# Up stages of two feed-forwards with the activations stationary and 512 weight columns moving

## Chip, cores and metric

One core of one Trainium2 chip. The metric is the device time of one execution in microseconds; the medians below are over runs of the same program.

## What is computed

One encoder layer on 256 tokens of width 2048 in float32: a SwiGLU feed-forward, token mixing by two kinds of attention heads, a second feed-forward. Each part has a normed and modulated input (adaLN) and a gated residual. The change touches the two feed-forwards:

```python
def swiglu(x, w_gate, w_up, w_down):
    return (jax.nn.silu(x @ w_gate) * (x @ w_up)) @ w_down

mod = jax.nn.silu(c) @ w_ada[l] + b_ada[l]
f = swiglu(modulate(rms_norm(h, g_ffn1[l]), sh1, sc1), w1_gate[l], w1_up[l], w1_down[l])
h = h + 0.5 * gt1[:, None, :] * f
```

D_FF is 5632; `w_gate` and `w_up` are 2048 x 5632, `w_down` 5632 x 2048, `w_ada` 2048 x 18432. 501 MB are read from HBM, all weights once.

## The kernel before

**Numbers.** A float32 matrix product is made of three fp32r products. Each operand is split in a high half (a cast to fp32r) and a low half (the rest). `mm3` (L212) issues high x high, high x low and low x high into the same PSUM bank; `mm2` (L217) does the same in two matmuls, the first of 512 columns that hold the high and the low half of the moving operand, the second of 256.

**The weight stream.** `Flow` (L50) streams all weights of the layer in the order of their use, in chunks of 128 x 1024 floats (512 KB): `fetch` issues the DMA on SP's queue (4 buffers), `to_hi` casts on ACT (L84, tile `hiw`, 4 buffers), `to_lo` subtracts on DVE (L91, tile `low`, 3 buffers). `step` (L114) is one chunk: high half of chunk u+3, low half of chunk u+2, then the events registered for this chunk (phase 0), then adaLN jobs, then the events of phase 1. What `step` returns is chunk u, on which PE works next. `fl.at(d, fn)` registers work for the d-th step from the coming one. So the order on each engine is written out by hand.

**adaLN jobs.** The 9 x 2048 values of `mod` are dot products on DVE (L186, 1024 columns of `w_ada` in each). They run beside the other work: at each step the credit grows by the rate of the stage (`RATE_A` to `RATE_H`), and for each whole credit one job runs, if its load has been issued (3 buffers). `pace` sets the rate and puts the credit to zero.

**Feed-forward.** The 16 k tiles of the input (`nh[k]`, `nl[k]`, 128 x 256: high and low half of the activations, channels on partitions) become ready one after another, so the sum over k is split in passes (SPLIT1 = 3, 8, 16; SPLIT2 = 4, 10, 16). `up_start` (L355) does the first k tiles for 8 f tiles, with all eight PSUM banks. `up_pass` (L370) runs over the f tiles (128 of D_FF each, FT = 44): per f one PSUM bank `pu` with gate in columns 0 to 255 and up in 256 to 511, per k one `mm3` for each. The stationary operand is the 128 x 128 block of weights, the moving one are the 256 tokens, and the result has D_FF on partitions. The first pass copies it to `part` (`keep`, ACT), the later ones add it there (DVE, L381). After the last pass `silu_soon` (L337) makes tanh (ACT), two products (DVE, L343 and L344), the high half (ACT) and the low half (DVE) of the hidden activations `hd`, one step after another. `ffn_down` (L388) takes them as the moving operand: per output tile 44 blocks, `mm2` each.

**Where the other form stands already.** `qkv_unit` (L556) has the activations stationary (128 tokens of `nh[k]`) and 512 columns of weights moving, with `mm3`; tokens are then on partitions.

```python
for t in range(2):
    ts_ = slice(t * P, (t + 1) * P)
    mm3(ps[t], nh[k][:, ts_], nl[k][:, ts_], whi[:, sl], wlo[:, sl],
        k == 0, k == KT - 1)
```

Transposes on PE stand in the attention heads (L646 and L688): a block of 128 x 128 float32 against `ident`.

Of the kernel before, what the change touches and what calls it, by code (L numbers as in the profile page):

```python
# [9 lines left out]
F32 = mybir.dt.float32  # L10
# [18 lines left out]
NF0 = 8  # L29
# [3 lines left out]
RATE_B = 0.66  # L33
RATE_C = 0.28
RATE_D = 0.97
# [14 lines left out]
class Flow:  # L50
# [63 lines left out]
    def step(self):  # L114
        u = self.u
        self.to_hi(u + LOOK + 1)
        self.to_lo(u + LOOK)
        self.run(0)
        self.credit += self.rate
        while self.credit >= 1.0 and self.fetched:  # L120
            self.credit -= 1.0
            self.job()
        self.run(1)
        self.u += 1
        return self.hi.pop(u), self.lo.pop(u)

    def next(self):
        if self.blk == 8:
            self.w = self.step()
            self.blk = 0  # L130
        sl = slice(self.blk * P, (self.blk + 1) * P)
        self.blk += 1
        return self.w[0][:, sl], self.w[1][:, sl]
# [7 lines left out]
def build(tc, a):  # L141
    nc = tc.nc
    with ExitStack() as ctx:
# [77 lines left out]
        def split_hi(src, hi):  # L221
            nc.scalar.copy(hi, src)
# [7 lines left out]
        def rstd_tiles(w, tag):  # L230
            return [sp.tile([P, w], F32, tag=f"{tag}{i}", bufs=(2 if i == 2 else 1), name=f"{tag}{i}") for i in range(3)]
# [18 lines left out]
        class Stat:  # L250
# [7 lines left out]
            def square(self, t, on_dve=False):  # L258
                sq = sp.tile([P, S], F32, tag="sq", bufs=3, name="sq")
                if on_dve:  # L260
                    nc.vector.tensor_tensor(sq, t, t, ALU.mult)
                else:
                    nc.scalar.activation(sq, t, AF.Square)
                return sq
# [60 lines left out]
        part, hid, pairs = {}, {}, {}  # L325

        def pair_tile(hp, kind, f, dt):
            key = kind, f // 2
            if key not in pairs:
                pairs[key] = hp.tile([P, 2, 2, S], dt, tag="hid", name=f"{kind}{f // 2}")  # L330
            return pairs[key][:, f % 2]

        def keep(hp, f, ps):
            part[f] = pair_tile(hp, "pt", f, F32)
            nc.scalar.copy(part[f], ps)  # L335

        def silu_soon(hp, f, d):  # L337

            g_, u_ = part[f][:, 0, :], part[f][:, 1, :]
            th = sp.tile([P, S], F32, tag="nt", bufs=4, name="th")  # L340

            def e1():
                nc.vector.scalar_tensor_tensor(th, th, 1.0, g_, ALU.add, ALU.mult)  # L343
                nc.vector.scalar_tensor_tensor(th, th, 0.5, u_, ALU.mult, ALU.mult)  # L344

            def e2():
                hid[f] = pair_tile(hp, "hd", f, F32R)
                split_hi(th, hid[f][:, 0, :])

            fl.at(d, lambda: nc.scalar.activation(th, g_, AF.Tanh, scale=0.5))  # L350
            fl.at(d + 1, e1)
            fl.at(d + 2, e2)
            fl.at(d + 3, lambda: split_lo(th, hid[f][:, 0, :], hid[f][:, 1, :]))

        def up_start(hp, K, before):  # L355
            pa = [bank(f"pa{f}").rearrange("p (j s) -> p j s", j=2) for f in range(NF0)]
            for k in range(K):
                for j in range(2):
                    whi, wlo = before(k, j)
                    assert k in normed  # L360
                    for b in range(8):
                        f, q = 4 * j + b // 2, b % 2
                        sl = slice(b * P, (b + 1) * P)
                        mm3(pa[f][:, q, :], whi[:, sl], wlo[:, sl], nh[k], nl[k],
                            k == 0 and q == 0, k == K - 1 and q == 1, skip_group_check=True)
                    if k == K - 1:
                        for f in range(4 * j, 4 * j + 4):
                            fl.at(0, lambda f=f: keep(hp, f, pa[f]))

        def up_pass(hp, f0, k0, k1, kind):  # L370
            for f in range(f0, FT):
                ps = bank("pu").rearrange("p (j s) -> p j s", j=2)
                for j in range(2):
                    for k in range(k0, k1):
                        w = fl.next()
                        assert k in normed, (f, k)
                        mm3(ps[:, j, :], *w, nh[k], nl[k], k == k0, k == k1 - 1)
                if kind == "first":
                    fl.at(0, lambda f=f, ps=ps: keep(hp, f, ps))
                else:  # L380
                    fl.at(0, lambda f=f, ps=ps: nc.vector.tensor_tensor(part[f], part[f], ps, ALU.add))  # L381
                    if kind == "last":
                        silu_soon(hp, f, 1)
# [32 lines left out]
        hp = hps.enter_context(tc.tile_pool(name="hid1", bufs=FT // 2 + 1))  # L416
        K1 = SPLIT1[0]

        def big(nm):
            return hp.tile([P, 4, S], F32, tag="hid", name=nm)  # L420
# [6 lines left out]
        def early_load(k):  # L427
            for j in (1, 0):
                for b in range(2):
                    early[k, j, b] = big("ra").rearrange("p a s -> p (a s)")  # L430
                    nc.sync.dma_start(early[k, j, b], a["w_ada"][j * KT + k, b])
# [5 lines left out]
        for k in range(1, K1):  # L437
            early_load(k)
            fl.fetch(min(2 * k + 1, RAWW - 1))
        for b in range(2):  # L440
            th = big("thc").rearrange("p a s -> p (a s)")
            cs = slice(b * CW, (b + 1) * CW)
            nc.scalar.activation(th, cb[:, cs], AF.Tanh, scale=0.5)
            nc.vector.scalar_tensor_tensor(cb[:, cs], th, 1.0, cb[:, cs], ALU.add, ALU.mult)
# [8 lines left out]
        for q in range(4):  # L453
            sq = big("sq1")
            nc.scalar.activation(sq, h4[q], AF.Square)
            for i in range(4):
                nc.tensor.matmul(ps1, ones, sq[:, i, :], start=q + i == 0, stop=q + i == 6)
# [29 lines left out]
        up_pass(hp, NF0, 0, K1, "first")  # L487
# [11 lines left out]
        pairs.clear()  # L499
# [268 lines left out]
        hp2 = ctx.enter_context(tc.tile_pool(name="hid2", bufs=FT // 2 + 1))  # L768
# [12 lines left out]
        up_pass(hp2, NF0, 0, K2, "first")  # L781
# [11 lines left out]
def _consts():  # L793
# [25 lines left out]
    "w1_s": (SPLIT1[0] * 2, P, CW), "w1_a": ((FT - NF0) * 2 * SPLIT1[0] // 8, P, CW),  # L819
    "w1_b": (FT * 2 * (SPLIT1[1] - SPLIT1[0]) // 8, P, CW),  # L820
    "w1_c": (FT * 2 * (SPLIT1[2] - SPLIT1[1]) // 8, P, CW), "w1_d": (KT * FT // 8, P, CW),
    "w2_s": (SPLIT2[0] * 2, P, CW), "w2_a": ((FT - NF0) * 2 * SPLIT2[0] // 8, P, CW),
# [7 lines left out]
def _arrays(inputs):  # L830
# [23 lines left out]

    arr["c"] = c(g["c"].reshape(2, CW))
    for l, cuts in ((1, SPLIT1), (2, SPLIT2)):
        gu = np.stack([g[f"w{l}_gate"][0], g[f"w{l}_up"][0]]).reshape(2, KT, P, FT, P)
        gu = gu.transpose(3, 0, 1, 2, 4)
        arr[f"w{l}_s"] = stream(gu[:NF0, :, : cuts[0]].transpose(2, 0, 1, 3, 4))
        arr[f"w{l}_a"] = stream(gu[NF0:, :, : cuts[0]])  # L860
        arr[f"w{l}_b"] = stream(gu[:, :, cuts[0] : cuts[1]])
        arr[f"w{l}_c"] = stream(gu[:, :, cuts[1] :])
# [24 lines left out]
```

## Time and profile before

| | |
|---|---|
| median of 3 runs | 1968.88 us (1966.86 to 1969.74) |
| profiled execution | 1968.11 us |
| its span, first to last instruction | 1966.3 us |
| PE busy | 1925.8 us, 98% |
| DVE busy | 1557.6 us, 79% |
| ACT busy | 900.2 us, 46% |
| HBM read | 501.14 MB, 256 GB/s over the span |

The matmuls of PE overlap: the next begins before the last one has ended, and their ends are modelled. So the duration of one matmul is longer than its share of the time, and the share is read from start to start, or from the pieces of the chain of waits. The chain goes back from the last instruction to what released each, so it shows what sets the end. An arrow `<-` names the instruction that ended an idle time; "issue" means that the profile shows no wait.

### The profile page before, as it was taken

To read this page: it belongs to the slowest core of one execution; us is meant where nothing else is said; L and a number is where in the kernel's file an instruction comes from. 1 tells how busy PE (TensorE), PEld (TensorE's weight loads), DVE (VectorE), ACT (ScalarE), POOL (GpSimd) and SP (SyncE) were. 2 spreads that over 40 slices of the span, in tenths; PEclk is the share of its full clock that TensorE was granted. 3 is DMA by queue.
4 is the path that set the end of the run, shared out by engine and by line. 5 is a ranking of instruction groups with operands and counts; after the bars stand their busy time and mean duration, and the time that the engine had idled before them with its cause. 6 is when DMAs were issued, how large, how long until landed. Compare 5 with 4: busy or idle time off the path is not lost.

```text
span 1966.3 us, 34176 instructions
## 1 busy us (share of the span) xinstructions
PE 1925.8 (98%) x13552; PEld 1805.0 (92%) x13552; DVE 1557.6 (79%) x2238; ACT 900.2 (46%) x1299; POOL 0.7 (0%) x6
## 2 busy tenths in 40 slices
PE   5999999999999999999999999999999999999999
PEld 4999999999988888788888998999999999988887
DVE  5889987888899999778888988777777889876444
ACT  3653334444443334455555544554333555533332
POOL 0000000000000000000000000000000000000000
PEclk8999999999999999999999999999999999999999
DMA  8898886777799999676766646888777666786553
GB/s 310 310 337 305 309 299 233 236 240 237 229 327 373 365 370 361 206 237 215 250 204 205 209 166 224 293 290 265 257 254 260 216 220 218 223 281 235 195 192 127
DMA packets 141137, 505.48 MB, mean 257 GB/s; under 512 B 15664, under 2 KB 17968, under 8 KB 140976
## 3 DMA queue, kind: packets, MB, share of 16 engines
q1 hardware_dynamic: 140976, 503.30, 74.9%
q8 instruction: 106, 1.74, 0.3%
q14 instruction: 55, 0.45, 0.1%
HBM read 501.14 MB, written 2.10 MB: 256 GB/s over the span
## 4 chain that ended last, share of the span: by engine, by line
PE 95%; DVE 3%; DMA 2%; issue 0%; ACT 0%; SPq 0%; DVEq 0%; ACTq 0%
PE pd L218 17%; PE pu L213 17%; PE pu L215 17%; PE pu L214 17%; PE pd L219 9%; PE pqv L213 2%; PE pqv L214 2%; PE pqv L215 2%; PE pqk L213 2%; PE pqq L213 1%; PE pqk L215 1%; PE pqq L215 1%; PE pqk L214 1%; PE pqq L214 1%; PE pso L213 1%; PE pso L215 1%
## 5 line engine op out<-in xcount | busy, mean ns | idle before, releaser
L84 ACT CAST hiw<-rw 128x1024 fp32r<-128x1024 f32 x656 | 691.9, 1056 | 997.2 <-PE pu L214 359.8
L91 DVE TENSOR_TENSOR low<-rw,hiw 128x1024 fp32r<-128x1024 f32 x656 | 802.4, 1224 | 346.7 <-issue 128.8
L213 PE MATMUL pu<-nx,hiw 128*128 128x256 f32 x2704 | 765.3, 283 | 0.2 <-ACT pt L335 0.2
L215 PE MATMUL pu<-nx,low 128*128 128x256 f32 x2704 | 765.2, 283 | 0.0
L214 PE MATMUL pu<-nx,hiw 128*128 128x256 f32 x2704 | 765.2, 283 | 0.0
L213 PEld LDWEIGHTS pu<-nx,hiw 128*128 128x128 f32 x2704 | 519.2, 192 | 0.4 <-ACT pt L335 0.4
L215 PEld LDWEIGHTS pu<-nx,low 128*128 128x128 f32 x2704 | 519.2, 192 | 0.0
L214 PEld LDWEIGHTS pu<-nx,hiw 128*128 128x128 f32 x2704 | 519.2, 192 | 0.0
L218 PE MATMUL pd<-hd,hiw 128*128 128x512 f32 x1408 | 497.6, 399 | 0.0
L219 PE MATMUL pd<-hd,low 128*128 128x256 f32 x1408 | 395.5, 281 | 0.0
L218 PEld LDWEIGHTS pd<-hd,hiw 128*128 128x128 f32 x1408 | 264.6, 188 | 65.8
L219 PEld LDWEIGHTS pd<-hd,low 128*128 128x128 f32 x1408 | 266.0, 189 | 0.0
L186 DVE CUSTOM_DVE_ANT_0 ra<-ra,cb,acc 128x1024 f32<-128x1024 f32 x144 | 187.1, 1299 | 0.2
L381 DVE TENSOR_TENSOR pt<-pt,pu 128x512 f32<-128x512 f32 x176 | 119.8, 681 | 0.0
L186 DVE CUSTOM_DVE_ANT_0 ra<-ra,cb,vec 128x1024 f32<-128x1024 f32 x64 | 81.8, 1279 | 0.0
L213 PE MATMUL pso<-ox,hiw 128*128 128x256 f32 x256 | 72.3, 282 | 0.0
L215 PE MATMUL pso<-ox,low 128*128 128x256 f32 x256 | 71.4, 279 | 0.0
L214 PE MATMUL pso<-ox,hiw 128*128 128x256 f32 x256 | 71.4, 279 | 0.0
L186 DVE CUSTOM_DVE_ANT_0 ra<-ra,cb,gin 128x1024 f32<-128x1024 f32 x48 | 64.3, 1341 | 0.0
L213 PE MATMUL pqv<-hiw,nx 128*128 128x512 f32 x128 | 51.5, 402 | 3.5 <-ACT nx L297 3.5
L213 PE MATMUL pqk<-hiw,nx 128*128 128x512 f32 x128 | 51.4, 401 | 0.0
L213 PE MATMUL pqq<-hiw,nx 128*128 128x512 f32 x128 | 50.9, 397 | 0.0
(128 smaller groups left out, 1676.9 us busy)
## 6 DMA issues: line engine op xcount, KB each, us to landing
ra<-in_w_ada_dram SPq DMA_DIRECT2D x288, 512.0 KB, 5.0
rw<-in_w_d_dram SPq DMA_DIRECT2D x176, 512.0 KB, 4.8
rw<-in_w_c_dram SPq DMA_DIRECT2D x154, 512.0 KB, 4.2
rw<-in_w_b_dram SPq DMA_DIRECT2D x121, 512.0 KB, 4.6
rw<-in_w_qkv_dram SPq DMA_DIRECT2D x96, 512.0 KB, 4.2
rw<-in_w_a_dram SPq DMA_DIRECT2D x63, 512.0 KB, 4.7
rw<-in_w_o_dram SPq DMA_DIRECT2D x32, 512.0 KB, 3.6
rw<-in_w_s_dram SPq DMA_DIRECT2D x14, 512.0 KB, 3.8
```

What stands on the lines that cost most here:

```text
L84: self.nc.scalar.copy(t, self.raw[self.nhi])
L91: self.nc.vector.tensor_tensor(t, self.raw.pop(self.nlo), self.hi[self.nlo].bitcast(F32), ALU.subtract)
L186: nc.vector.tensor_tensor_reduce(out=raw, in0=raw, in1=cb[:, b * CW : (b + 1) * CW], scale=scale, scalar=init, op0=ALU.mult, op1=ALU.add, ...
L213: nc.tensor.matmul(out, lh, rh, start=first, stop=False, **kw)
L214: nc.tensor.matmul(out, lh, rl, start=False, stop=False, **kw)
L215: nc.tensor.matmul(out, ll, rh, start=False, stop=last, **kw)
L218: nc.tensor.matmul(ps, lh, r.rearrange("p t s -> p (t s)"), start=first, stop=False)
L219: nc.tensor.matmul(ps[:, :S], ll, r[:, 0, :], start=False, stop=last)
L381: fl.at(0, lambda f=f, ps=ps: nc.vector.tensor_tensor(part[f], part[f], ps, ALU.add))
```

## The change

Gate and up projections take the form that the q/k/v projection has. `wide3` multiplies 128 tokens (stationary) by 512 weight columns (moving), for both halves of the tokens; the four weight tiles of a group G share one such matmul, and gate and up (j = 0, 1) follow one another in two banks each. The weights are laid out for this on the host (`halves`). `part[G]` holds tokens on partitions: two halves of 512 columns, for gate and for up. `gate_soon` makes tanh and the first product as soon as gate is complete; `hid_soon` makes the second product (`e0`, DVE), turns it by eight transposes on PE into two banks `ph` (`e1`, in a new phase 3 of the step, just ahead of the chunk's matmuls), and splits it from there (`e2` on ACT, `e3` on DVE) into the same `hid[f]` as before, four f tiles in one tile. The down projection is as before. Tiles of the pool `hid` are twice as big and half as many; `sq` shares two buffers with tanh, and the tiles of `rstd_tiles` share `nt`. Three rates are changed.

```diff
-NF0 = 8
-RATE_B = 0.66
-RATE_C = 0.28
-RATE_D = 0.97
+RATE_B = 0.6
+RATE_C = 0.36
+RATE_D = 0.9
...
         self.run(1)
+        self.run(3)
         self.u += 1
...
+    def half(self):
+        w = self.blk
+        if w == 8:
+            self.w = self.step()
+            w = 0
+        self.blk = w + 4
+        sl = slice(w * P, (w + 4) * P)
         return self.w[0][:, sl], self.w[1][:, sl]
...
-            return [sp.tile([P, w], F32, tag=f"{tag}{i}", bufs=(2 if i == 2 else 1), name=f"{tag}{i}") for i in range(3)]
+            ts = [sp.tile([P, S], F32, tag="nt", bufs=4, name="rt")[:, :w] for i in range(2)]
+            return ts + [sp.tile([P, w], F32, tag=tag, bufs=2, name=tag)]
...
-                sq = sp.tile([P, S], F32, tag="sq", bufs=3, name="sq")
+                sq = sp.tile([P, 512], F32, tag="th", bufs=2, name="sq")[:, :S]
...
-        part, hid, pairs = {}, {}, {}
-
-        def pair_tile(hp, kind, f, dt):
-            key = kind, f // 2
-            if key not in pairs:
-                pairs[key] = hp.tile([P, 2, 2, S], dt, tag="hid", name=f"{kind}{f // 2}")
-            return pairs[key][:, f % 2]
-
-        def keep(hp, f, ps):
-            part[f] = pair_tile(hp, "pt", f, F32)
-            nc.scalar.copy(part[f], ps)
-
-        def silu_soon(hp, f, d):
-
-            g_, u_ = part[f][:, 0, :], part[f][:, 1, :]
-            th = sp.tile([P, S], F32, tag="nt", bufs=4, name="th")
+        part, hid = {}, {}
+
+        def wide3(ps, k, whi, wlo, first, last):
+            assert k in normed, k
+            for t in range(2):
+                ts_ = slice(t * P, (t + 1) * P)
+                mm3(ps[t], nh[k][:, ts_], nl[k][:, ts_], whi, wlo, first, last)
+
+        def keep(hp, G, j, ps):
+            if j == 0:
+                part[G] = hp.tile([P, 2, 2, 512], F32, tag="hid", name=f"pt{G}")
+            for t in range(2):
+                nc.scalar.copy(part[G][:, j, t, :], ps[t])
+
+        def add(G, j, ps):
+            for t in range(2):
+                nc.vector.tensor_tensor(part[G][:, j, t, :], part[G][:, j, t, :], ps[t], ALU.add)
+
+        def gate_soon(G, d):
+            pt = part[G]
+            ths = [sp.tile([P, 512], F32, tag="th", bufs=2, name="th") for t in range(2)]
+
+            def e0():
+                for t in range(2):
+                    nc.scalar.activation(ths[t], pt[:, 0, t, :], AF.Tanh, scale=0.5)
 
             def e1():
-                nc.vector.scalar_tensor_tensor(th, th, 1.0, g_, ALU.add, ALU.mult)
-                nc.vector.scalar_tensor_tensor(th, th, 0.5, u_, ALU.mult, ALU.mult)
+                for t in range(2):
+                    nc.vector.scalar_tensor_tensor(pt[:, 0, t, :], ths[t], 1.0, pt[:, 0, t, :], ALU.add, ALU.mult)
+
+            fl.at(d, e0)
+            fl.at(d + 1, e1)
+
+        def hid_soon(hp, G, d):
+            pt = part[G]
+            box = {}
+
+            def e0():
+                for t in range(2):
+                    nc.vector.scalar_tensor_tensor(
+                        pt[:, 0, t, :], pt[:, 0, t, :], 0.5, pt[:, 1, t, :], ALU.mult, ALU.mult)
+
+            def e1():
+                for i in range(2):
+                    box[i] = bank("ph").rearrange("p (f s) -> p f s", f=2)
+                    for f in range(2):
+                        cs = slice((2 * i + f) * P, (2 * i + f + 1) * P)
+                        for t in range(2):
+                            nc.tensor.transpose(box[i][:, f, t * P : (t + 1) * P], pt[:, 0, t, cs], ident)
 
             def e2():
-                hid[f] = pair_tile(hp, "hd", f, F32R)
-                split_hi(th, hid[f][:, 0, :])
-
-            fl.at(d, lambda: nc.scalar.activation(th, g_, AF.Tanh, scale=0.5))
-            fl.at(d + 1, e1)
+                q = hp.tile([P, 4, 2, S], F32R, tag="hid", name=f"hd{G}")
+                box["q"] = q
+                for i in range(2):
+                    nc.scalar.copy(q[:, 2 * i : 2 * i + 2, 0, :], box[i])
+                for f in range(4):
+                    hid[4 * G + f] = q[:, f]
+
+            def e3():
+                q = box["q"]
+                for i in range(2):
+                    nc.vector.tensor_tensor(
+                        q[:, 2 * i : 2 * i + 2, 1, :], box[i], q[:, 2 * i : 2 * i + 2, 0, :].bitcast(F32), ALU.subtract)
+
+            fl.at(d, e0)
+            fl.at(d + 1, e1, 3)
             fl.at(d + 2, e2)
-            fl.at(d + 3, lambda: split_lo(th, hid[f][:, 0, :], hid[f][:, 1, :]))
+            fl.at(d + 3, e3)
 
         def up_start(hp, K, before):
-            pa = [bank(f"pa{f}").rearrange("p (j s) -> p j s", j=2) for f in range(NF0)]
+            pa = [[[bank(f"pa{G}") for t in range(2)] for j in range(2)] for G in range(2)]
             for k in range(K):
+                for G in range(2):
+                    whi, wlo = before(k, G)
+                    for j in range(2):
+                        sl = slice(j * 512, (j + 1) * 512)
+                        wide3(pa[G][j], k, whi[:, sl], wlo[:, sl], k == 0, k == K - 1)
+                    if k == K - 1:
+                        for j in range(2):
+                            fl.at(0, lambda G=G, j=j: keep(hp, G, j, pa[G][j]))
+
+        def up_pass(hp, G0, k0, k1, kind):
+            for G in range(G0, FT // 4):
                 for j in range(2):
-                    whi, wlo = before(k, j)
-                    assert k in normed
-                    for b in range(8):
-                        f, q = 4 * j + b // 2, b % 2
-                        sl = slice(b * P, (b + 1) * P)
-                        mm3(pa[f][:, q, :], whi[:, sl], wlo[:, sl], nh[k], nl[k],
-                            k == 0 and q == 0, k == K - 1 and q == 1, skip_group_check=True)
-                    if k == K - 1:
-                        for f in range(4 * j, 4 * j + 4):
-                            fl.at(0, lambda f=f: keep(hp, f, pa[f]))
-
-        def up_pass(hp, f0, k0, k1, kind):
-            for f in range(f0, FT):
-                ps = bank("pu").rearrange("p (j s) -> p j s", j=2)
-                for j in range(2):
+                    ps = [bank("pu") for t in range(2)]
                     for k in range(k0, k1):
-                        w = fl.next()
-                        assert k in normed, (f, k)
-                        mm3(ps[:, j, :], *w, nh[k], nl[k], k == k0, k == k1 - 1)
-                if kind == "first":
-                    fl.at(0, lambda f=f, ps=ps: keep(hp, f, ps))
-                else:
-                    fl.at(0, lambda f=f, ps=ps: nc.vector.tensor_tensor(part[f], part[f], ps, ALU.add))
+                        wide3(ps, k, *fl.half(), k == k0, k == k1 - 1)
+                    if kind == "first":
+                        fl.at(0, lambda G=G, j=j, ps=ps: keep(hp, G, j, ps))
+                        continue
+                    fl.at(0, lambda G=G, j=j, ps=ps: add(G, j, ps))
                     if kind == "last":
-                        silu_soon(hp, f, 1)
+                        (hid_soon(hp, G, 1) if j else gate_soon(G, 1))
 
...
-        hp = hps.enter_context(tc.tile_pool(name="hid1", bufs=FT // 2 + 1))
+        hp = hps.enter_context(tc.tile_pool(name="hid1", bufs=FT // 4 + 1))
...
-            return hp.tile([P, 4, S], F32, tag="hid", name=nm)
+            return hp.tile([P, 8, S], F32, tag="hid", name=nm)
...
-        up_pass(hp, NF0, 0, K1, "first")
+        up_pass(hp, 2, 0, K1, "first")
...
+    def halves(units):
+        return c(units.reshape(-1, 2, P, 512).transpose(0, 2, 1, 3).reshape(-1, P, CW))
...
-        gu = np.stack([g[f"w{l}_gate"][0], g[f"w{l}_up"][0]]).reshape(2, KT, P, FT, P)
+        gu = np.stack([g[f"w{l}_gate"][0], g[f"w{l}_up"][0]]).reshape(2, KT, P, FT // 4, 512)
-        arr[f"w{l}_s"] = stream(gu[:NF0, :, : cuts[0]].transpose(2, 0, 1, 3, 4))
-        arr[f"w{l}_a"] = stream(gu[NF0:, :, : cuts[0]])
-        arr[f"w{l}_b"] = stream(gu[:, :, cuts[0] : cuts[1]])
-        arr[f"w{l}_c"] = stream(gu[:, :, cuts[1] :])
+        arr[f"w{l}_s"] = halves(gu[:2, :, : cuts[0]].transpose(2, 0, 1, 3, 4))
+        arr[f"w{l}_a"] = halves(gu[2:, :, : cuts[0]])
+        arr[f"w{l}_b"] = halves(gu[:, :, cuts[0] : cuts[1]])
+        arr[f"w{l}_c"] = halves(gu[:, :, cuts[1] :])
```

## Rows read from the trace of the kernel before

**Rows 1.** The page: span; busy time of each engine; shares of the chain that ended last.

```profile
span 1966.3 us, 34176 instructions
PE 1925.8 (98%) x13552; PEld 1805.0 (92%) x13552; DVE 1557.6 (79%) x2238; ACT 900.2 (46%) x1299; POOL 0.7 (0%) x6
...
PE 95%; DVE 3%; DMA 2%; issue 0%; ACT 0%; SPq 0%; DVEq 0%; ACTq 0%
```

**Rows 2.** Waits of PE, all stages: us in total, times, longest.

```profile
PE pa L215 <- DVE low L91: 2.0, 3, 0.8
...
PE pu L213 <- ACT pt L335: 0.2, 1, 0.2
```

**Rows 3.** Chain of waits, up stage, 43 pieces: start, length, what; first and last.

```profile
298.93 0.12 PE pu L214
...
303.97 0.12 PE pu L214
```

**Rows 4.** Chain at the end of the first start stage.

```profile
49.53 4.34 DMA rw<-in_w_a_dram
...
55.56 0.39 PE pu L213
```

**Rows 5.** Timeline of PE where the first down projection begins.

```profile
545.25 0.40 PE L218 MATMUL pd<-hd,hiw 128*128 128x512 f32 x1
```

**Rows 6.** Chain, q/k/v projection without attention beside it, 28 pieces: first and last.

```profile
868.78 0.23 PE pqv L213
...
874.90 0.23 PE pqv L213
```

**Rows 7.** Timeline of PE around four transposes in the q/k/v stage.

```profile
936.08 0.39 PE L215 MATMUL pqq<-hiw,nx 128*128 128x512 f32 x1
936.31 0.60 PE L688 MATMUL pP<-ident,sc 128*128 128x128 f32 x4
...
939.49 0.39 PE L213 MATMUL pqq<-hiw,nx 128*128 128x512 f32 x1
```

**Rows 8.** Groups by line: the transposes of the attention weights, mean ns of one.

```profile
L688 PE MATMUL pP<-ident,sc 128*128 128x128 f32 x64 | 9.6, 272 | 0.0
```

**Rows 9.** Timeline of DVE in the last pass of the first up stage.

```profile
401.50 1.23 DVE L91 TENSOR_TENSOR low<-rw,hiw 128x1024 fp32r<-128x1024 f32 x1 [1.65 <-PE pu L215]
402.64 0.42 DVE L225 TENSOR_TENSOR hd<-th,hd 128x256 fp32r<-128x256 f32 x1
...
403.78 0.68 DVE L381 TENSOR_TENSOR pt<-pt,pu 128x512 f32<-128x512 f32 x1
404.38 1.23 DVE L91 TENSOR_TENSOR low<-rw,hiw 128x1024 fp32r<-128x1024 f32 x1
405.53 1.28 DVE L186 CUSTOM_DVE_ANT_0 ra<-ra,cb,gat 128x1024 f32<-128x1024 f32 x1
...
407.26 1.22 DVE L91 TENSOR_TENSOR low<-rw,hiw 128x1024 fp32r<-128x1024 f32 x1 [0.45 <-issue]
```

**Rows 10.** Stretches (first pass, last pass, down projection): busy us by engine, clock, DMA, GB/s.

```profile
56.00:133.00 77.00, 77.00 (x644) 77.00 (x643) 65.88 (x84) 49.57 (x72) 0.00 (x0) 1.00 0.92 332
292.00:545.00 253.00, 253.00 (x2110) 253.00 (x2110) 205.76 (x307) 120.58 (x174) 0.00 (x0) 1.00 0.71 236
546.00:790.00 244.00, 244.00 (x1383) 211.63 (x1383) 226.55 (x305) 98.12 (x106) 0.00 (x0) 1.00 0.97 362
```

**Rows 11.** Timeline of DVE at the end of the output projection.

```profile
1195.33 0.42 DVE L275 TENSOR_TENSOR sqa<-sqa,sq 128x256 f32<-128x256 f32 x1
1195.81 1.23 DVE L91 TENSOR_TENSOR low<-rw,hiw 128x1024 fp32r<-128x1024 f32 x1
```

**Rows 12.** Waits of PE in the output projection's stretch.

```profile
PE pstat L281 <- DVE sqa L275: 0.8, 1, 0.8
```

**Rows 13.** Timeline of PE in the first down projection, nine pairs between these rows.

```profile
599.66 0.40 PE L218 MATMUL pd<-hd,hiw 128*128 128x512 f32 x1
...
602.84 0.40 PE L218 MATMUL pd<-hd,hiw 128*128 128x512 f32 x1
```

More of the change, by code (lines that the diff above doesn't have):

```diff
@@ L132, in next @@
         self.blk += 1
+        return self.w[0][:, sl], self.w[1][:, sl]
+    def half(self):
[5 more added lines that the diff above has]
+        sl = slice(w * P, (w + 4) * P)
         return self.w[0][:, sl], self.w[1][:, sl]
@@ L428, in early_load @@
             for j in (1, 0):
+                t = big("ra")
                 for b in range(2):
-                    early[k, j, b] = big("ra").rearrange("p a s -> p (a s)")
+                    early[k, j, b] = t[:, 4 * b : 4 * b + 4, :].rearrange("p a s -> p (a s)")
                     nc.sync.dma_start(early[k, j, b], a["w_ada"][j * KT + k, b])
@@ L439, in build @@
             fl.fetch(min(2 * k + 1, RAWW - 1))
+        thc = big("thc")
         for b in range(2):
-            th = big("thc").rearrange("p a s -> p (a s)")
+            th = thc[:, 4 * b : 4 * b + 4, :].rearrange("p a s -> p (a s)")
             cs = slice(b * CW, (b + 1) * CW)
@@ L453, in build @@
         for q in range(4):
-            sq = big("sq1")
+            if q % 2 == 0:
+                sq8 = big("sq1")
+            sq = sq8[:, 4 * (q % 2) : 4 * (q % 2) + 4, :]
             nc.scalar.activation(sq, h4[q], AF.Square)
@@ L498, in build @@
         hid.clear()
-        pairs.clear()
         hps.close()
@@ L767, in build @@
         K2 = SPLIT2[0]
-        hp2 = ctx.enter_context(tc.tile_pool(name="hid2", bufs=FT // 2 + 1))
+        hp2 = ctx.enter_context(tc.tile_pool(name="hid2", bufs=FT // 4 + 1))
         mod_jobs(range(K2, KT), 7, 6, r3)
@@ L780, in build @@
         up_start(hp2, K2, before2)
-        up_pass(hp2, NF0, 0, K2, "first")
+        up_pass(hp2, 2, 0, K2, "first")
         fl.pace(RATE_F)
@@ L818 @@
     "x": (4, P, 4, S), "w_ada": (9 * KT, 2, P, CW), "vecs": (P, 224), "c": (2, CW),
-    "w1_s": (SPLIT1[0] * 2, P, CW), "w1_a": ((FT - NF0) * 2 * SPLIT1[0] // 8, P, CW),
+    "w1_s": (SPLIT1[0] * 2, P, CW), "w1_a": ((FT - 8) * 2 * SPLIT1[0] // 8, P, CW),
     "w1_b": (FT * 2 * (SPLIT1[1] - SPLIT1[0]) // 8, P, CW),
     "w1_c": (FT * 2 * (SPLIT1[2] - SPLIT1[1]) // 8, P, CW), "w1_d": (KT * FT // 8, P, CW),
-    "w2_s": (SPLIT2[0] * 2, P, CW), "w2_a": ((FT - NF0) * 2 * SPLIT2[0] // 8, P, CW),
+    "w2_s": (SPLIT2[0] * 2, P, CW), "w2_a": ((FT - 8) * 2 * SPLIT2[0] // 8, P, CW),
     "w2_b": (FT * 2 * (SPLIT2[1] - SPLIT2[0]) // 8, P, CW),
```

## Prediction

> **What bounds the kernel now.** I read the page first. The reader is to see that PE is busy 1925.8 of 1966.3 us and holds 95% of the chain that ended last [rows 1]. A busy PE is not yet a PE at its peak, so the second view is what PE waits for: in the up stages next to nothing, 0.2 us at the first `pu` matmul and 2.0 us for the low halves in the two start stages [rows 2]. The third view is the chain of waits inside an up stage. It is an unbroken row of matmuls, and their slot is the number that matters: from 298.93 to 303.97 us there are 42 steps, so one matmul of 256 columns takes 5.04 / 42 = 0.1200 us [rows 3]. The whole stage says the same: 4080 `pu` matmuls lie between 55.56 us, where the first starts, and 545.25 us, where the first down projection starts, 0.1200 us each [rows 4, 5]. There is no idle time to remove; what counts is how long PE needs for a column, and what new work it gets.
>
> **The wide form.** The q/k/v projection already has it: `nx` stationary, 512 columns of `hiw` or `low` moving, the same three products. There 27 steps take 874.90 - 868.78 = 6.12 us, 0.2267 us each [rows 6]. Two narrow slots cost 0.2400, so a merged pair saves 0.0133 us. I take the wide slot for the up stages because stationary operand, moving operand, types and order of the products are the same.
> Counts: gate and up have 44 x 2 x 16 = 1408 blocks in each feed-forward, three products each, 4224 narrow matmuls; after the change 2112 wide ones. In the first feed-forward 144 of the 4224 stand in `up_start`, whose end waits for a DMA (4.34 us from 49.53 us on, then ACT, then PE at 55.56 us [rows 4]); I count no gain there (at most 72 x 0.0133 = 1 us). So it gains 2040 x 0.01333 = 27.2 us, and the second feed-forward, which has no such wait at that point, 2112 x 0.01333 = 28.2 us. Together **-55.4 us**.
>
> **The transposes.** New on PE: 8 per group of four f tiles, 11 groups, two feed-forwards, 176 in all. The trace has the same operation, an f32 128 x 128 block against the identity, in bursts of four. From the matmul at 936.08 us to the one at 939.49 us there are 13 slots of 512 columns and one burst: 3.41 - 13 x 0.2267 = 0.463 us for four, the slightly longer slots just behind the burst included [rows 7]. 44 bursts cost **+20.4 us**, all of it on the path, for PE has no idle time to hide it.
> The same row shows a mean duration of 272 ns for one transpose [rows 8]; these ends overlap, so I don't take it, but it is the upper bound: 176 x 0.272 = 47.9 us. Below 0.1 us each I see no row.
> The Trainium skill, in "TensorE: Matmul & The Clock Gate", Part 4: PE-mode transpose, gives about 275 ns for one 128 x 128 transpose in a kernel's context and puts most of it down to access latency. By it the sum would lose almost the whole gain; the burst in the trace speaks against it.
>
> **A wait that PE did not have.** `e1`, the transposes, now needs what DVE has made in `e0`. Behind the transposes on PE stand the matmuls of the next chunk, and behind these everything else. DVE is not free to run ahead: the low half of a later chunk waits for PE to give back the buffer of an earlier one (the 1.65 us at 401.50 us), so DVE's work of a chunk begins when PE begins the chunk, here every 2.88 us (401.50, 404.38, 407.26) [rows 9]. From start to start on DVE: a low half 1.14 us, an operation of 512 elements 0.60 (its own length is 0.68), an adaLN reduction 1.28 [rows 9]. After the change a chunk is 12 wide slots, 2.72 us. Let PE end group G at time 0. In the first chunk DVE does a low half and two adds, to 2.34; at 2.72 the next low half, to 3.86; then `e0`, two operations, to 3.86 + 0.60 + 0.68 = 5.14. The transposes stand at 5.44: 0.3 us to spare. If the first chunk also holds an adaLN job, DVE is at 3.62 instead, at 4.76 after the low half and at 6.04 after `e0`: PE waits 0.60 us.
> How often? The credit of a pass grows by the rate in each chunk from zero, and a job runs when it passes a whole number. Groups end after 8 chunks in the first feed-forward (rate 0.36) and after 6 in the second (rate 0.2, unchanged). The chunk behind a group's end holds a job 5 times in the first (chunks 9, 17, 25, 73, 81) and twice in the second (25, 55). In the second, a job in the chunk before it (30 and 60), beside `e1` of the gate, leaves about 0.35 us of lag, twice. 7 x 0.60 + 2 x 0.35 = **+4.9 us**. Bounds: 0, if the operations end sooner than I add up, and 22 x 0.60 = 13.2, if each group is late.
>
> **Rates and streams.** In the first pass RATE_A stays 0.9 while a chunk shrinks from 2.88 to 2.72 us: 1.9 loads of 524288 bytes in 2.72 us are 366 GB/s, where the stretch moved 332 [rows 10]. The down projection moved 362 GB/s at a DMA share of 0.97 and PE had no idle time in it [rows 10], so this just fits. I take **+1 us**, bounds 0 and 4. DVE's share in the last pass was 205.76 of 253 us [rows 10]; the wide form gives it fewer and longer operations and the shorter chunk less time. No bound by itself, since a low half may be over 3 us late before PE starves.
> RATE_B, C and D sum to fewer jobs: 32, 31 and 77 where 36, 24 and 83 stood. So 32 jobs are left behind the first feed-forward, not 29, and in the attention stages a thirtieth one now falls in the 112th chunk counted from RATE_Q, at the end of the output projection. There DVE has 0.14 us of idle time (an add starts at 1195.33, its successor 0.34 later could, the low half starts at 1195.81 [rows 11]) and PE already waits 0.8 us for DVE's sums [rows 12]. One job of 1.28 us puts **+1.1 us** on the path there; lower bound 0.
>
> **Parts at nothing.** PSUM adds and copies: as many of 512 elements as before. The product, its halves and tanh go from pieces of 256 to pieces of 512, hidden behind PE; their price without that cover is the wait above. `ph` takes two of the eight banks, free again two chunks later; two banks for `pu` where one stood, for twice the time between. `sq` with two buffers, not three, holds ACT until DVE's sum in the same chunk; ACT is at 46% [rows 1] and its next high half has a chunk of slack. The last group's `hid` is due in the sixth chunk of the down projection and DVE ends it about 0.4 us before. Down, q/k/v and attention stay as they are.
>
> **Sum.** -55.4 + 20.4 + 4.9 + 1.0 + 1.1 = -28.0 us: a span of 1938.3 us. Outside its span the profiled execution has 1968.1 - 1966.3 = 1.8 us: 1940.1. It lies 0.8 us below the median of the runs: **1941 us**, 1.4% faster.
>
> **Rivals.**
> First, DVE late at every group, not at nine: a job's backlog carried from chunk to chunk, 1.0 us a group. 22.0 instead of 4.9: 1958 us. For it: DVE is the second busiest engine [rows 1]. Against: each chunk's sum above stays under 2.72 us without a job.
> Second, transposes that do not overlap beside 512-column matmuls, by the mean of 272 ns [rows 8]: +27.5 us, 1968 us, no change. This is also what the Trainium skill's figure would make of it. Against: the burst of four in 0.463 us, between the same kind of matmuls [rows 7].
> Third, slower: the wide slot of the up stage is not that of q/k/v but that of the down projection. There a pair of 512 and 256 columns takes (602.84 - 599.66) / 9 = 0.3533 us [rows 13]; split by columns the long one takes 0.2356. On 4152 wide matmuls 0.0089 more is +37 us: 1978 us. The point from which it decides is 0.0133 x 4152 less 27.4 of new costs, a slot of 0.2334. For it: that stage is a feed-forward with the same engines beside it. Against: it alternates long and short matmuls, and where the form is uniform the slot is 0.2267.
>
> **How the numbers follow.** Forecast 0.80; late at every group 0.07; transposes at full length 0.05; the slower slot 0.05; under the range 0.03. The range takes the bounds of the forecast: without wait, DMA cost and extra job, and with 1 us from the first start stage, 1933; with every group 0.60 late and 4 us of DMA, 1952. I give 1932 to 1953. A measurement of this kernel tells about 0.2%, 4 us, from no change: faster 0.90, same 0.05, slower 0.05.
>
> **What would show it.** Right: `pu` slots of 0.227 us in the chain; bursts of eight transposes under 1 us; PE waits of some 0.6 us at the transposes, released by DVE, nine or so of 22; the first pass of 73 to 77 us. Wrong: slots above 0.233, PE waits on DVE at every group, or low halves that PE waits for in the first pass because DMA is at its limit.

## The result and the profile after

The changed kernel takes 1939.76 us (median of 4 runs, 1939.11 to 1940.54) against 1969.31 us: ratio 0.9855, 95% interval 0.9842 to 0.9867. The forecast was 1941. The span of the profiled execution is 1938.2 us, forecast 1938.3.

The page after: span, busy time, shares of the chain. PE is still the engine that sets the end [rows 1], with 9504 matmuls where 13552 stood.

```profile
span 1938.2 us, 25880 instructions
PE 1894.9 (98%) x9504; PEld 1604.2 (83%) x9504; DVE 1537.9 (79%) x2106; ACT 889.5 (46%) x1211; POOL 0.7 (0%) x6
...
PE 93%; DVE 5%; DMA 1%; issue 1%; ACT 0%; SPq 0%; DVEq 0%; ACTq 0%
```

The chain of waits in the up stage after, 23 pieces, first and last, to be held against [rows 3]: 22 steps in 4.98 us, a slot (from one matmul's start to the next) of 0.226 us. Read over stretches of 20 us without transposes it is 0.2267, that of the q/k/v projection [rows 6].

```profile
298.93 0.23 PE pu L222
...
303.91 0.23 PE pu L223
```

PE's waits after (us in total, times, longest). The new line is `ph`, seven times, on DVE's product.

```profile
PE po L223 <- DVE pl L234: 3.0, 2, 2.8
...
PE ph L383 <- DVE pt L374: 1.6, 7, 0.3
PE pstat L291 <- DVE sqa L285: 1.4, 1, 1.4
```

Two bursts of eight transposes on PE's timeline, a late one at 306 us and one in time at 376.

```profile
306.02 0.39 PE L224 MATMUL pu<-hiw,nx 128*128 128x512 f32 x1
306.35 0.30 PE L383 MATMUL ph<-ident,pt 128*128 128x128 f32 x1
306.86 0.99 PE L383 MATMUL ph<-ident,pt 128*128 128x128 f32 x7 [0.21 <-DVE pt L374]
307.60 0.48 PE L222 MATMUL pu<-hiw,nx 128*128 128x512 f32 x1
...
375.72 0.40 PE L224 MATMUL pu<-hiw,nx 128*128 128x512 f32 x1
375.95 1.04 PE L383 MATMUL ph<-ident,pt 128*128 128x128 f32 x8
376.75 0.48 PE L222 MATMUL pu<-hiw,nx 128*128 128x512 f32 x1
```

From the wide matmul ahead of a burst to the twelfth behind it, less twelve slots of 0.2267 us, the burst in time costs 0.90 us and the late one 1.48. Read so for the 20 groups that have wide matmuls behind them, 11 cost 0.90 to 0.92, seven 1.47 to 1.54 and two 1.08 and 1.11. The seven stand where the prediction had put a job behind the group's end, the two where a job stands one chunk earlier.

Why the late one is late, on DVE's timeline. The group ends where the low half at 300.83 us begins. The adds follow, then a job (303.17), then the next low half (304.38), and only then the product (L374), which ends at 306.80. In [rows 9] DVE worked by the same rule (low half, registered events, job), but no matmul waited for the end of a product.

```profile
300.83 1.22 DVE L90 TENSOR_TENSOR low<-rw,hiw 128x1024 fp32r<-128x1024 f32 x1 [1.50 <-PE pu L223]
301.98 1.28 DVE L351 TENSOR_TENSOR pt<-pt,pu 128x512 f32<-128x512 f32 x2
303.17 1.28 DVE L195 CUSTOM_DVE_ANT_0 ra<-ra,cb,gat 128x1024 f32<-128x1024 f32 x1
304.38 0.08 DVE L195 DVE_READ_ACCUMULATOR2_ANT acc<- 128x1 f32 x1
304.38 1.22 DVE L90 TENSOR_TENSOR low<-rw,hiw 128x1024 fp32r<-128x1024 f32 x1
305.51 1.29 DVE L374 SCALAR_TENSOR_TENSOR pt<-pt 128x512 f32<-128x512 f32 x2
```

Stage by stage, each from the start of its first matmul to that of the next stage, in us (the prediction's terms beside it):

| stage | before | after | difference | predicted |
|---|---|---|---|---|
| up to the first `pu` | 55.56 | 56.01 | +0.45 | 0 |
| up passes 1 | 489.69 | 474.38 | -15.3 | -27.2, ten bursts, 5 waits, +1 DMA: -14 |
| down 1, to the norm's first matmul | 248.75 | 249.60 | +0.85 | one burst, +0.9 |
| norm, q/k/v, attention, output | 410.81 | 413.49 | +2.7 | +1.1 |
| start stage 2 | 24.83 | 23.44 | -1.4 | -1.3 |
| up passes 2 | 483.84 | 467.58 | -16.3 | -26.9, ten bursts, 4 waits: -15.7 |
| down 2, to its last matmul | 248.64 | 249.49 | +0.85 | one burst, +0.9 |

The rows of the two start stages can't be read to better than about 1 us. The runs told below that have the same code there put the first `pu` between 54.95 and 56.76 us, and give 23.44 to 24.44 us for start stage 2. So neither the +0.45 nor the agreement at -1.4 can be told from scatter.

### The profile page after: what moved, and what is told of

It reads as the page before. It is cut to its first block, busy times and chain, and to the rows that moved or that the text cites. A ratio compares the mean times of both kernels' runs of the same rounds, so it can differ in the third digit from the quotient of the medians.

```text
span 1938.2 us, 25880 instructions
## 1 busy us (share of the span) xinstructions
PE 1894.9 (98%) x9504; PEld 1604.2 (83%) x9504; DVE 1537.9 (79%) x2106; ACT 889.5 (46%) x1211; POOL 0.7 (0%) x6
## 4 chain that ended last, share of the span: by engine, by line
PE 93%; DVE 5%; DMA 1%; issue 1%; ACT 0%; SPq 0%; DVEq 0%; ACTq 0%
PE pd L227 17%; PE pu L222 16%; PE pu L224 16%; PE pu L223 16%; PE pd L228 9%; PE pqv L222 2%; DVE low L90 2%; PE pqv L223 2%; PE pqv L224 2%; PE pqk L222 2%; PE pqq L222 2%; PE pqk L224 2%; PE pqk L223 2%; PE pqq L224 2%; PE pqq L223 2%; PE ph L383 1%
## 5 line engine op out<-in xcount | busy, mean ns | idle before, releaser
L222 PE MATMUL pu<-hiw,nx 128*128 128x512 f32 x1352 | 527.8, 390 | 0.0
L224 PE MATMUL pu<-hiw,nx 128*128 128x512 f32 x1352 | 526.3, 389 | 0.0
L223 PE MATMUL pu<-low,nx 128*128 128x512 f32 x1352 | 526.1, 389 | 0.0
L224 PEld LDWEIGHTS pu<-hiw,nx 128*128 128x128 f32 x1352 | 253.8, 188 | 52.9
L223 PEld LDWEIGHTS pu<-low,nx 128*128 128x128 f32 x1352 | 253.8, 188 | 52.3
L222 PEld LDWEIGHTS pu<-hiw,nx 128*128 128x128 f32 x1352 | 253.8, 188 | 52.0
L351 DVE TENSOR_TENSOR pt<-pt,pu 128x512 f32<-128x512 f32 x176 | 112.4, 680 | 0.0
L222 PE MATMUL pqq<-hiw,nx 128*128 128x512 f32 x128 | 50.8, 397 | 0.0
```

The costliest lines, as they stand in the source:

```text
L222: nc.tensor.matmul(out, lh, rh, start=first, stop=False, **kw)
L223: nc.tensor.matmul(out, lh, rl, start=False, stop=False, **kw)
L224: nc.tensor.matmul(out, ll, rh, start=False, stop=last, **kw)
L351: nc.vector.tensor_tensor(part[G][:, j, t, :], part[G][:, j, t, :], ps[t], ALU.add)
```

## The experiments

**Without the turn.** What do the transposes cost, and the waits in front of them?

```diff
             fl.at(d, e0)
-            fl.at(d + 1, e1, 3)
+            box[0], box[1] = (pt[:, 0, i, :].rearrange("p (f s) -> p f s", f=2) for i in range(2))
```

> The changed kernel without its 176 transposes: the high and low halves of the hidden activations are taken straight from the product in part, in the wrong layout, so the turn is the part that is left out; all else is the same. Theory (the turn is serial on PE, 0.907 us per group of eight, and nine groups wait for the product besides, 7 times 0.57 us and twice 0.18): 22 x 0.907 + 7 x 0.57 + 2 x 0.18 = 24.3 us less, 1915.5 us. Rival (the turn is mostly hidden in the weight loads around it, and what is gained by wide matmuls is small): less than 8 us less, over 1931 us. Second rival (transposes at their full 272 ns): 48 us less, 1892 us.

Measured: 1915.29 us (ratio to before 0.9730, 0.9714 to 0.9746), 24.5 us under the changed kernel. The two up stages take 462.54 and 456.96 us, 27.15 and 26.88 less than before, which is the slot's term with nothing else in it. The turn is serial on PE at 0.11 us a transpose; the rival of a hidden turn would have left more than 1931 us, the one at 272 ns 1892 us.

**Half the width.** Is the gain one of width?

```diff
-                mm3(ps[t], nh[k][:, ts_], nl[k][:, ts_], whi, wlo, first, last)
+                for n, (st, mv) in enumerate(((nh, whi), (nh, wlo), (nl, whi))):
+                    for c in range(2):
+                        cs = slice(c * S, (c + 1) * S)
+                        nc.tensor.matmul(
+                            ps[t][:, cs], st[k][:, ts_], mv[:, cs], start=first and n + c == 0,
+                            stop=last and n + c == 3, skip_group_check=True)
```

> The changed kernel with each of its 512-column matmuls in the up stages cut in two of 256 columns, both with the same stationary activations; transposes and everything else stay. Theory (each matmul has a fixed part of 0.0133 us, whichever operand is stationary, and the gain of the change is that half of these parts go): 4152 x 0.0133 = 55.4 us more, less about 2 us because the longer chunk leaves DVE more time before the transposes: 1993 us, and up-stage slots of 0.120 us. Rival (the gain comes from having the activations stationary, the same block loaded again and again, not from the width): slots of 0.1133 us and about 1940 us. Between them, the slot of the output projection in the kernel before, 0.1178 us: 1975 us.

Measured: 1990.56 us (1.0113, 1.0098 to 1.0128), 50.8 us over the changed kernel. Its chain in the up stage is one piece of 43 matmuls in 5.16 us, 0.120 us each, and no transpose waits any more, as the longer chunk would have it:

```profile
298.93 5.16 PE pu L344 x43
```

So with these tiles where they lie, swapping the operands gains nothing by itself; the width does. The runs on placement, below, limit this.

**The product one chunk earlier.** Do the waits come from DVE's order?

```diff
-            fl.at(d, e0)
+            fl.at(d - 1, e0)
             fl.at(d + 1, e1, 3)
```

> The second product of a group is issued on DVE in the chunk of the add, right behind the add and ahead of that chunk's adaLN job and of the next low half, not one chunk later. Theory (the waits of PE at the transposes come from a job and a low half that stand ahead of the product in DVE's order): DVE ends the product 3.6 us after the group's end, the transposes stand at 5.44, so all nine waits go: 7 x 0.57 + 2 x 0.18 = 4.3 us less, 1935.4 us, and no PE wait on the product. Rival (the waits are an effect of DVE's total load and come back somewhere else, as late low halves): 1939 to 1941 us, PE waits on low halves in the last passes.

Measured: 1935.43 us (0.9831, 0.9816 to 0.9845), 4.3 us under the changed kernel. Each of the 20 bursts costs 0.90 to 0.91 us, and there is no wait at `ph`. The same group on DVE: adds, product, then the job and two low halves, with nothing late behind them.

```profile
301.09 1.28 DVE L351 TENSOR_TENSOR pt<-pt,pu 128x512 f32<-128x512 f32 x2
302.28 1.29 DVE L374 SCALAR_TENSOR_TENSOR pt<-pt 128x512 f32<-128x512 f32 x2
303.49 1.28 DVE L195 CUSTOM_DVE_ANT_0 ra<-ra,cb,gat 128x1024 f32<-128x1024 f32 x1
304.69 0.09 DVE L195 DVE_READ_ACCUMULATOR2_ANT acc<- 128x1 f32 x1
304.69 2.36 DVE L90 TENSOR_TENSOR low<-rw,hiw 128x1024 fp32r<-128x1024 f32 x2
```

**The old rates.**

```diff
-RATE_B = 0.6
-RATE_C = 0.36
-RATE_D = 0.9
+RATE_B = 0.66
+RATE_C = 0.28
+RATE_D = 0.97
```

> The changed kernel with the three adaLN rates of the kernel before (0.66, 0.28, 0.97). Theory (rates act only through which chunks hold a job): by the credit, 3 groups of the first feed-forward have a job in the chunk behind their end, not 5, so 2 x 0.57 us less, and the job at the end of the output projection goes, 0.6 us less: about 1938 us; the down projection's loads of 365 GB/s still fit. Rival (the new rates were needed, because at the shorter chunk DVE or DMA starves PE in the second pass or in the down projection): 1943 us or more, with PE waits on low halves there.

Measured: 1938.26 us (0.9844, 0.9830 to 0.9859). The waits moved as the credits said, five at the transposes instead of seven, and 0.7 us at the end of the output projection instead of 1.4:

```profile
PE ph L383 <- DVE pt L374: 1.2, 5, 0.3
PE pstat L291 <- DVE sqa L285: 0.7, 1, 0.7
```

The difference of 1.5 us between the medians is below what these runs can tell. What they do tell is that the new rates were not needed: nothing starves with the old ones.

**More load in the first pass.**

```diff
-RATE_A = 0.9
+RATE_A = 1.0
```

> The changed kernel with an adaLN job in every chunk of the first pass (RATE_A 1.0, not 0.9): two loads of 524288 bytes in each 2.72 us are 385 GB/s. The first pass moved 347 GB/s at a DMA share of 0.95, and the down projection before the change 362 at 0.97, so full share would be some 365 to 373. Theory (the first pass stands just under the DMA limit, which is why my 1 us for it was not paid): at 370 GB/s 27 chunks need 76.5 us, not 73.4, so PE waits some 1 to 3 us there; three jobs fewer are left later, so the job at the end of the output projection goes, 0.6 us less. 1940 to 1942 us. Rival (loads in flight and buffers cover a pass as short as this): no PE wait in the first pass, 1939 us.

Measured: 1938.89 us (0.9846, 0.9829 to 0.9862): the rival. The stretch of the first pass (busy us of PE, weight loads, DVE, ACT, POOL; clock; DMA share; GB/s), in the changed kernel and in this one:

```profile
56.00:129.40 73.40, 73.40 (x325) 60.80 (x324) 66.10 (x86) 49.07 (x71) 0.00 (x0) 1.00 0.95 347
```

```profile
56.00:129.40 73.40, 73.40 (x325) 60.81 (x324) 69.38 (x92) 50.08 (x75) 0.00 (x0) 1.00 0.97 367
```

367 GB/s, and PE has no idle time. Whether the loads would run short in a pass longer than 73 us was not tried.

**Early product and RATE_D 0.95.**

```diff
-RATE_D = 0.9
+RATE_D = 0.95
...
-            fl.at(d, e0)
+            fl.at(d - 1, e0)
```

> The early product as in the run before, and RATE_D 0.95 in place of 0.9, so that 28 jobs are left behind the first feed-forward and none falls in the 112th chunk of the attention stages. Theory: PE's wait for DVE's sums at the end of the output projection goes from 1.4 back to 0.8 us; 1934.8 us, and no PE wait at the transposes. Rival (that wait is due to the shared buffers of the squares, not to the extra job): it stays at 1.4 us, 1935.4 us.

Measured: 1934.06 us (0.9823, 0.9808 to 0.9837). The wait at the end of the output projection is 0.7 us: it hung on the job, not on the shared buffers. With the shift of all tiles by 64 bytes, told below, this is the best of the versions in the wide form.

**Where the tiles lie.** The attention part had lost 2.7 us, and 0.6 of them was the extra job. Something else was new: `pso`, whose code is untouched, had gone from slots of 0.1178 us to 0.1200. The change makes the pools ahead of the attention tiles 1088 bytes smaller, and `ox`, its moving operand, starts at byte 32 of 128 where it had started at byte 96; the weight halves start at byte 32 in both. All of the following stand on the version just told, but for the one that says otherwise.

```diff
+            pad = ac.tile([P, 16], F32, name="pad")
+            nc.vector.memset(pad, 0.0)
             gq = ac.tile([P, 4, HD], F32, name="gq")
```

> The version with early product and RATE_D 0.95, and a tile of 64 bytes per partition ahead of the attention stages' tiles, so that the moving operand of the output projection starts at byte 96 of 128, as in the kernel before, not at byte 32, where the change has put it by making the pools ahead of it smaller. The output projection's code was not changed, but its 256-column slot went from 0.1178 to 0.1200 us. Theory (the start of the moving operand sets this): 0.1178 us again, 768 x 0.0022 = 1.7 us less. Rival (the slot goes with something else, such as the instruction stream or the run): 0.1200 us.

Measured: 1934.74 us, one run, which tells nothing at this size. The slot answers: over the 359 last matmuls of the projection it is 0.1177 us here, 0.1200 in the changed kernel. So 64 bytes move it. In the timeline it shows as 26 steps of 3.12 us in all in the changed kernel, and of 3.06 us here:

```profile
1149.76 0.28 PE L222 MATMUL pso<-ox,hiw 128*128 128x256 f32 x1
...
1152.88 0.28 PE L224 MATMUL pso<-ox,low 128*128 128x256 f32 x1
```

```profile
1149.75 0.28 PE L223 MATMUL pso<-ox,hiw 128*128 128x256 f32 x1
...
1152.81 0.28 PE L222 MATMUL pso<-ox,hiw 128*128 128x256 f32 x1
```

Next, all tiles together: 16 columns ahead of them, then 24.

```diff
+        pad = cp.tile([P, 16], F32, name="pad")
+        nc.vector.memset(pad, 0.0)
         epst = cp.tile([P, 1], F32, name="epst")
```

> The same version with the 64 bytes ahead of all tiles, so that the activations, the weight halves and the attention tiles all start at byte 96 of 128, not 32. Theory (a start at byte 32 costs a little in each matmul whose operands lie there): the output projection's slot 0.1178 us, 1.7 us less; and if the same holds for 512 columns, some 0.002 us less for each of 5376 wide matmuls, 10 us, 1924 us. Rival (the wide slot of 0.2267 us does not hang on it): 1932 to 1934 us.

> The same with 96 bytes ahead of all tiles, so that all start at byte 0 of 128. Theory (the start within 128 bytes counts and 0 is the best): the output projection's slot at most 0.1178 us and at most 1932 us; with an effect on 512 columns as well, 1924 us. Rival (no effect of placement on PE): 1934 us, the slot of the output projection 0.1200 us.

Measured: 1933.87 us (0.9826, 0.9812 to 0.9841) and 1935.62 us (0.9835, 0.9819 to 0.9852); `pso` at 0.1200 and `pu` at 0.2267 us in both. The theory of both expectations fell: with both operands at the same byte, 32, 96 or 0, the slots are the same. What was left to try was their distance. So the activations were moved against the weights, in the wide form by 64 and by 32 bytes, and in the kernel before by 64:

```diff
+        pad = cp.tile([P, 16], F32, name="pad")
+        nc.vector.memset(pad, 0.0)
         nx = [cp.tile([P, 2, S], F32R, tag=f"nx{k}", name=f"nx{k}") for k in range(KT)]
+        pad2 = cp.tile([P, 16], F32, name="pad2")
+        nc.vector.memset(pad2, 0.0)
```

(Shown for a distance of 64; for 32 the two tiles have 8 and 24 columns. The wide ones also have the 64 bytes ahead of `gq`.)

> The version with early product and RATE_D 0.95, with 64 bytes so placed that the activations and the attention results start at byte 96 of 128 while the weight halves stay at byte 32. The three placements before this one showed the output projection at 0.1177 us where its two operands lie 64 bytes apart within 128, and at 0.1200 where both start at the same byte, whichever that is. Theory (the distance counts, and only where the weight load limits the slot): output projection 0.1178 us, 1.7 us less; the wide slot stays at 0.2267: 1932 us. Rival (the distance counts for each matmul): wide slot 0.2245, 9 us less on top, 1923 us.

Measured: 1944.23 us (0.9880, 0.9864 to 0.9897; runs from 1942.7 to 1949.6), some 10 us slower than without. Neither theory: the wide slot grew. The chain in the first up stage (23 pieces) and in the second (22):

```profile
298.81 0.23 PE pu L227
...
303.84 0.23 PE pu L228
...
1400.00 0.23 PE pu L226
...
1404.90 0.23 PE pu L226
```

5.03 / 22 = 0.229 and 4.90 / 21 = 0.2333 us; read over stretches of 20 us it is 0.2289 throughout the first feed-forward, 0.2333 in the second up to some 1520 us, and 0.2289 behind that.

> The kernel before with nothing changed but 64 bytes ahead of and behind the activation tiles, so that they start at byte 96 of 128 while the weight halves stay at byte 32. Theory (two operands 64 bytes apart make the narrow slot 0.1178 us, as in its output projection): the up stages' slot 0.1178, 8448 x 0.0022 = 18.6 us less, 1950 us, so a good half of what the change gained could have been had this way. Rival (the up stage's 0.1200 us has another cause): 0.1200 us and 1968.5 us.

Measured: 1923.1 us (0.9762, 0.9718 to 0.9806; runs of 1907.0, 1921.6, 1924.6 and 1928.6): far more than the theory's 1950, and faster than the changed kernel, without any change to its work. The chain in the two up stages (44 and 45 pieces):

```profile
298.92 0.12 PE pu L218
...
303.99 0.12 PE pu L219
...
1399.98 0.11 PE pu L218
...
1404.97 0.11 PE pu L217
```

5.07 / 43 = 0.1179 us in the first feed-forward, as expected, and 4.99 / 44 = 0.1134 in the second. The pairs of the down projection went from 0.3533 [rows 13] to 0.3467 us as well, nine pairs in 3.12 us, though both of their operands had moved by the same 128 bytes:

```profile
599.86 0.39 PE L222 MATMUL pd<-hd,hiw 128*128 128x512 f32 x1
...
602.98 0.39 PE L222 MATMUL pd<-hd,hiw 128*128 128x512 f32 x1
```

The changed kernel holds the opposite case. There `hd` starts at byte 96, with the weight halves at byte 32, where both had started at byte 32; yet the down projection kept its time (248.74 us without the turn, 248.75 before). So for the pairs the distance did not count. The q/k/v projection, wide and unchanged in this run, went the way of the wide form, from 0.2267 [rows 6] to 7.78 / 34 = 0.2288 us:

```profile
852.99 0.23 PE pqv L217
...
860.77 0.23 PE pqv L218
```

> As the placement before this with activations and weight halves 64 bytes apart within 128, which made the wide slot 0.2289 to 0.2333 us in place of 0.2267, but 32 bytes apart. Theory (the slot grows with the distance of the two operands): 0.2267 to 0.2289 us, 1932 to 1942 us. Rival (some distance is better than none for the wide form too, as 64 bytes was for the narrow one, which went to 0.1178 and 0.1133 us): a slot of 0.2200 us, 5376 x 0.0067 = 36 us less than the version at distance 0: some 1897 us. Second rival (a multiple of 32 that is not one of 64 counts as no distance): 0.2267 us and 1932 to 1934 us.

Measured: 1965.89 us (0.9988, 0.9978 to 0.9998), none of the three: with 32 bytes the slot is longer than it was with 64 in the first up stage. The chain in the first up stage has 22 pieces, 4.90 / 21 = 0.2333 us.

```profile
298.87 0.24 PE pu L226
...
303.77 0.24 PE pu L226
```

With this the whole gain of the change is gone, by 32 bytes.

## Why the prediction was right, and where it was not

**The slot of the wide form, -55.4 us.** Right in size, and the step that carried the sum: 0.2267 us, as in the q/k/v projection, and 54.0 us of it shown by the up stages of the run without the turn. But the reason given (same operands, types and order) was not enough. The q/k/v projection of the kernel before uses the same tiles, at the same bytes, as the up stages after the change; that the slot could be carried over hung on that too, and the prediction did not see it. The third rival, a slot from 0.2334 us on, was a real danger with another cause than the one named: it needed no alternation of long and short matmuls, only another start of a tile. And 0.0133 us per matmul is no constant of the form. The wide and the narrow slot at the same byte differ by 0.2267 - 0.1200 = 0.1067 us for 256 columns, which is 256 steps at 2.4 GHz (the granted clock of these stretches is 1.00). Over 0.1067 and 0.2133 us, a narrow matmul took 0.0133, 0.0111 or 0.0067 us more, a wide one 0.0133, 0.0156 or 0.0200.

**The transposes, +20.4 us.** Right: 22 bursts at 0.907, 20.0 us, and 24.5 with the waits when they are taken away. The rival with 272 ns fell by that run. The Trainium skill's "TensorE: Matmul & The Clock Gate", Part 4: PE-mode transpose, gives about 275 ns for a transpose in one kernel's context. As a duration that agrees with the 272 ns of [rows 8]; as a cost it does not, for in a burst of eight a transpose cost 0.113 us here, and the measurement decides.

**The wait on DVE, +4.9 us.** Right in place and cause, group by group; 7 x 0.58 + 0.2 + 0.2 = 4.4 us by the bursts, 4.3 by the run that removes them. The 0.35 us for the two smaller ones was too big by nearly half; they came out at 0.2.

**The first pass, +1 us.** Nothing was paid: PE's idle time there is zero, also at 367 GB/s. That DMA share reads 0.92 in [rows 10] is no sign of a limit near by.

**The attention part, +1.1 us.** The one term that was too small: +2.7. The job's share was 0.6, since PE's wait grew from 0.8 [rows 12] to 1.4 us, not by a whole job. The rest is in two things that the prediction did not look for. One is the slot of `pso`, worth about 1 us: the run that put it back at 0.1177 us took 0.9 us less in this part. The other is a stretch at half clock behind an old wait, worth about 1.5 us, as told next. The norm and the q/k/v projection took 0.4 us less. Just behind PE's longest wait for `pl` (3.0 us before, 2.8 after), the five microseconds read, before and after:

```profile
1151.70:1156.70 5.00, 4.99 (x40) 4.89 (x41) 3.69 (x6) 2.18 (x5) 0.00 (x0) 1.00 0.42 152
```

```profile
1137.40:1142.40 5.00, 5.00 (x29) 5.00 (x30) 2.26 (x4) 0.75 (x2) 0.00 (x0) 0.66 0.45 162
```

The granted clock is 1.00 and 0.66, that is, part of the stretch ran at 1.2 GHz instead of 2.4; 29 matmuls in place of 40. From the end of that wait to the next norm's first matmul it took 5.02 to 5.07 us in the profiles of the runs with old rates, higher RATE_A, early product and the first three placements, which show the fall too, and 3.58 us in those without the turn and with half the width, which do not. (Of the three profiles with activations moved against the weights, the wide one at 64 bytes shows it, the other two do not.) PE's wait was 2.7 to 2.9 us in all of them, so its length does not tell the two apart, and what decides was not tried.

That the span came out within 0.1 us is partly luck: the first pass (-1.0), the waits (-0.5) and the turn (-0.4) were over-priced by about what the attention part (+1.6) was under-priced, and the rest lies within the scatter of the start stages.

## What to carry to other kernels

A change of form is best priced by the same form elsewhere in the same trace, from start to start, with what its interruptions cost included; but see that the operands are the same tiles at the same places, for in these runs the price went with them. When work that was off the path becomes a thing that PE waits for, write down the order of that engine's instructions chunk by chunk: the waits, their number and their length follow from it, and so does the cheap cure (issue it before the work that can wait). Before a loop is turned around for a slot that is some per cent too long, move one operand by 64 bytes and measure: here that alone gave 1923.1 us, 17 us less than the turned loop, while the same move made the turned loop itself some 10 us slower.

## What was not expected of the hardware

The slot of a matmul with the same shape, types and order took different values in kernels that differ only in where tiles start in SBUF: 256 columns 0.1200, 0.1178 or 0.1133 us, 512 columns 0.2267, 0.2289 or 0.2333. With both operands at the same byte of 128 (32, 96 or 0) the values were 0.1200 and 0.2267. With 64 bytes between them the narrow form, weights stationary, got shorter (0.1178, 0.1133), and the wide form, weights moving, longer (0.2289, 0.2333); with 32 bytes the wide form had 0.2333. The down projection, whose matmuls alternate between 512 and 256 columns, does not fit. 64 bytes left its pairs at 0.3533 us. Where both of its operands moved by 128 bytes together, the pairs took 0.3467 us in the kernel before, but stayed at 0.3533 in the two wide kernels. Two things stay open. Within one execution the slot changed with no change of address (0.1178 and 0.1133 in the two feed-forwards, 0.2289 and 0.2333 in the other kernel), so there is a second cause beside placement. The spread of 1907 to 1929 us may be the same thing, but only the run of 1921.6 us has a profile. And moving the activations also moved all tiles behind them by 128 bytes, which was not tried by itself, so distance within 128 is a description of these runs, not a rule, and why the slot goes with placement is not shown. Whether the wide form has a placement with a shorter slot than 0.2267 was not found.
